# Two unused tiles ahead of the matmul operands: moving tile starts to multiples of 512 bytes

## The chip, the cores and the metric

The kernel is one program on one core of a Trainium2 chip. The metric is the device time of one execution in microseconds (us). The kernel before has a median of 947.3 us over three runs (946.58 to 951.47).

## The reference, cut to what matters

One layer of a hybrid decoder on 512 tokens of 1024 channels in float32: half a SwiGLU feed-forward step, a mixer of two groups (a convolution of 31 taps with a layer norm, and a gated linear recurrence), another half feed-forward step, and a last RMS norm.

```
def swiglu_ffn(x, w_gate, w_up, w_down):
    return (jax.nn.silu(x @ w_gate) * (x @ w_up)) @ w_down

x = x + 0.5 * swiglu_ffn(rmsnorm(x, ffn1_norm), ffn1_w_gate, ffn1_w_up, ffn1_w_down)
x = x + hybrid_mixer(rmsnorm(x, mix_norm), w_in, ..., w_out)
x = x + 0.5 * swiglu_ffn(rmsnorm(x, ffn2_norm), ffn2_w_gate, ffn2_w_up, ffn2_w_down)
y = rmsnorm(x, final_norm)
```

The inner width of the feed-forward steps is 2816, that is 22 feature tiles of 128. The mixer's input product has 2048 outputs, its output product 1024.

## The kernel before, in words

Every large product is made of three matmuls in float32r (a 4-byte type that TensorE reads in one pass). Both operands are split into a high part, rounded to float32r, and a low part, the rest; the product is high by high, high by low and low by high, all added up in one PSUM bank.

There are two kinds of these matmuls. In `mm_feat` (line 194) the weights are stationary and the tokens move: the stationary operand is a block of 128 by 128 of a weight slab `hl`, the moving operand a row of 512 or 256 tokens of `h_hi` or `h_lo`, the normed and transposed input. One unit is 24 such matmuls, 8 blocks times 3 products, into one bank (`pgate`, `pup` in the feed-forward steps, `pz` in the mixer). In `mm_tok` (lines 329, 330, 331) the activations are stationary and the weights move: the stationary operand is a block of 128 by 128 of an `act`, `uhi`, `ulo`, `yhi` or `ylo` tile, the moving operand 512 columns of a slab `hl`. Its outputs are called `pd`, and `pdl` at the program's end.

Counted in the built program, the 4656 float32r matmuls are 1584 of `mm_feat` with 512 columns, 1056 of `mm_feat` with 256 columns into `pgate` and `pup` (the first units, and those of the second feed-forward step that take half of the tokens at a time), 768 with 256 columns into `pz`, and 1248 of `mm_tok`, all with 512 columns.

A weight slab goes through three stages: a DMA of 512 KB into a tile `raw` (SyncE's queue), a cast of ScalarE into the high half of `hl` (line 119), and a subtraction on VectorE or GpSimd into its low half (line 133). Three `raw` and five `hl` tiles are in rotation, and the program writes these stages ahead of the unit that uses the slab by fixed numbers of units. The order on each engine comes from the order of the code and from priorities that the program gives to chains of small steps (norms, the convolution, the recurrence).

The tiles come from pools that lay them out one behind the other in each partition of the on-chip memory, in the order of the pools: first the persistent tiles (`const`), then `raw` and `hl`, then the working tiles, `act` among them. A tile's place is the sum of the sizes ahead of it, each rounded up to 32 bytes. So nothing is computed or moved by a tile that nobody reads or writes; it shifts what lies behind it.

| tile | byte in the partition, before | remainder by 512 | role in the large matmuls |
|---|---|---|---|
| `xt0` to `xt3` | 16512 and on | 128 | none |
| `h_hi`, `h_lo` | 32896, 49280 | 128 | moving in `mm_feat` |
| `ident`, `ones` | 65664, 66176 | 128 | none |
| `raw` | 88544 and on | 480 | none (DMA target) |
| `hl` | 100832 and on | 480 | stationary in `mm_feat`, moving in `mm_tok` |
| `act`, `uhi`, `ulo`, `yhi`, `ylo` | 149984 and on | 480 | stationary in `mm_tok` |

The blocks that one matmul reads begin at whole multiples of 512 bytes within their tile, so a tile's remainder is that of all its blocks.

Of the kernel before, what the change touches and what calls it, by code (L numbers as in the profile page):

```python
# [13 lines left out]
P = 128  # L14
# [44 lines left out]
def layer_kernel(ctx: ExitStack, tc, x, gains, w_g1, w_u1, w_d1a, w_d1b, w_in,  # L59
# [16 lines left out]
    def const(shape, name, dt=F32):  # L76
        return cp.tile(shape, dt, name=name, tag=name)

# [1 line left out]
    xt = [const([P, D], f"xt{t}") for t in range(4)]  # L80
    h_hi = const([P, KT, T], "h_hi", F32R)
    h_lo = const([P, KT, T], "h_lo", F32R)
    ident = const([P, P], "ident")
    ones = const([P, P], "ones")
    neghalf = const([P, 1], "neghalf")
# [16 lines left out]
        nc.sync.dma_start(g, gains[i:i + 1, :].broadcast_to([P, D]))  # L102
        return g

# [1 line left out]
    clock = {"pe": 0.0, "dve": 0.0, "pool": 0.0}  # L106
    chains, convs, done = [], [], {}

    def dve(us):
        clock["dve"] = max(clock["dve"], clock["pe"] - 3.0) + us  # L110

    # slabs are loaded, then split into two parts of float32r
    def slab_load(st, src):
        st["raw"] = wp.tile([P, D], F32, name=nm("raw"), tag="raw", bufs=RAW_BUFS)
        nc.sync.dma_start(st["raw"], src)
# [69 lines left out]
            if evac is not None:  # L185
                evac()

# [1 line left out]
    def mm_feat(ps, hl, t0, n):  # L189
        w = hl.rearrange("p s (k f) -> p s k f", k=KT)  # L190
        seq = [(0, h_hi), (0, h_lo), (1, h_hi)]
        for s, (a, h) in enumerate(seq):
            for k in range(KT):
                PE.matmul(ps, w[:, a, k, :], h[:, k, t0:t0 + n],  # L194
                          start=(s == 0 and k == 0), stop=(s == 2 and k == KT - 1))
# [5 lines left out]
            tc.keep_in_program_order(ins)  # L201
        return ins

    # a bank for the products beside the main ones
    def side_tile(name):
        if "free" in done:
            return pd.tile([P, T], F32, name=nm(name), tag="pd")
        return pp.tile([P, T], F32, name=nm(name), tag="pg")

# [1 line left out]
    def m4(name, dt=F32):  # L211
        return sp.tile([P, 4, HT], dt, name=nm(name), tag="act", bufs=ACT_BUFS)

# [58 lines left out]
        if key is not None:  # L272
            done[key] = True

# [1 line left out]
    def ffn_units(acts, j, wg, wu, parts, shared=False):  # L276
        box = {}

        def gate(t0, n, hl):
            if hl is not None:  # L280
                box["g"] = hl
            pg = pp.tile([P, T], F32, name=nm("pgate"), tag="pg")
            mm_feat(pg[:, :n], box["g"], t0, n)
            box["pg"] = pg

        def gate_out(t0, n):
            pg = box["pg"]
            sg = sp.tile([P, T], F32, name=nm("sg"), tag="sg", bufs=2)
            S.activation(sg[:, :n], pg[:, :n], AF.Silu)  # L289
            box["s"] = sg  # L290

        def up(t0, n, hl):
            if hl is not None:
                box["u"] = hl
            pu = pp.tile([P, T], F32, name=nm("pup"), tag="pg")
            mm_feat(pu[:, :n], box["u"], t0, n)
            box["pu"] = pu

        def up_out(t0, n):
            pu = box["pu"]  # L300
            sg = box["s"]
            act = acts[j]
            V.tensor_mul(sg[:, :n], pu[:, :n], sg[:, :n])  # L303
            S.copy(act[:, 0, t0:t0 + n], sg[:, :n])
            V.tensor_sub(act[:, 1, t0:t0 + n], sg[:, :n], act[:, 0, t0:t0 + n].bitcast(F32))  # L305
            dve(0.8 if n == 256 else 1.3)

        out_ = []
        for i, (t0, n) in enumerate(parts):
            us = 5.12 * n / 512  # L310
            out_.append((wg[j] if i == 0 else None, shared, us,
                         lambda hl, t0=t0, n=n: gate(t0, n, hl),
                         lambda t0=t0, n=n: gate_out(t0, n)))
            out_.append((wu[j] if i == 0 else None, shared, us,
                         lambda hl, t0=t0, n=n: up(t0, n, hl),
                         lambda t0=t0, n=n: up_out(t0, n)))
        return out_
# [6 lines left out]
            self[j] = new_act()  # L324
            return self[j]

# [1 line left out]
    def mm_tok(ps, ahi, alo, whi, wlo, first, last):  # L328
        PE.matmul(ps, ahi, whi, start=first, stop=False)  # L329
        PE.matmul(ps, ahi, wlo, start=False, stop=False)  # L330
        PE.matmul(ps, alo, whi, start=False, stop=last)  # L331
# [7 lines left out]
    def pd_tile():  # L339
        return pd.tile([P, 512], F32, name=nm("pd"), tag="pd")  # L340

    # down products of the first group of feature tiles, one half of the
    # output columns at a time, all tokens
    def down_a_units(wd, acts):
        box = {}

        def unit(oh, kp, hl):
            if kp == 0:
                box["ps"] = [pd_tile() for _ in range(4)]
            ps = box["ps"]  # L350
            hv = hl.rearrange("p s (j d) -> p s j d", j=2)
            for j in range(2):
                k = 2 * kp + j
                for t in range(4):
                    ts_ = slice(t * P, (t + 1) * P)
                    mm_tok(ps[t], acts[k][:, 0, ts_], acts[k][:, 1, ts_],
                           hv[:, 0, j, :], hv[:, 1, j, :], k == 0, k == NA - 1)

        def fin(oh):
            for t in range(4):  # L360
                add_res(t, oh, box["ps"][t], 0.5)

        return [(wd[oh, kp], False, 5.12, lambda hl, oh=oh, kp=kp: unit(oh, kp, hl),
                 (lambda oh=oh: fin(oh)) if kp == NA // 2 - 1 else None)
                for oh in range(2) for kp in range(NA // 2)]

    # products of two token tiles with the full width of the output
    def pair_units(ws, order, kept, left, toks, scale, shared, after, again=False):
        box = {}
        n = len(order)  # L370

        def unit(i, k, hl):
            if hl is None:
                hl = kept.pop(k)
            elif k in kept:
                kept[k] = hl
            if i == 0:
                done.pop("free", None)
                box["ps"] = [[pd_tile() for _ in range(2)] for _ in range(2)]
            ps = box["ps"]  # L380
            for j in range(2):
                hi, lo = left(k, j)
                for oh in range(2):
                    os_ = slice(oh * 512, (oh + 1) * 512)
                    mm_tok(ps[j][oh], hi, lo, hl[:, 0, os_], hl[:, 1, os_], i == 0, i == n - 1)

        def fin():
            for i, t in enumerate(toks):
                for oh in range(2):
                    add_res(t, oh, box["ps"][i][oh], scale)  # L390
            done["free"] = True
            after()

        return [(None if again and k in kept else ws[k], shared, 2.56,
                 lambda hl, i=i, k=k: unit(i, k, hl), fin if i == n - 1 else None)
                for i, k in enumerate(order)]
# [12 lines left out]
        order = [4, 5, 6, 7, 0, 1, 2, 3] if (YF0, YF1)[half] else list(range(8))  # L409
        return pair_units(w_out, order, {}, left, (2 * half, 2 * half + 1), 1.0, True, after)  # L410

# [1 line left out]
    def par(c, i):  # L413
        return ch[:, c, i:i + 1]

# [93 lines left out]
                    yield 0.4  # L509
        chains.append((PR_LN, layernorm(cv, half)))  # L510

    # mean over the channels, the same in every partition
    def channel_mean(v, box):
        ps2 = sp.tile([P, 2, HT], F32, name=nm("ps2"), tag="sg", bufs=2)
        V.tensor_add(ps2, v[:, 0:2, :], v[:, 2:4, :])
        V.tensor_add(ps2[:, 0, :], ps2[:, 0, :], ps2[:, 1, :])
        dve(1.1)
        for _ in range(NY3):
            yield 1
        pm = side_tile("pm")  # L520
        PE.matmul(pm[:, :HT], ones, ps2[:, 0, :], start=True, stop=True)
        box.append(pm)
# [106 lines left out]
        V.tensor_scalar_mul(psp, q, 8.0)  # L629
        V.tensor_scalar_mul(nsp, q, -8.0)  # L630

# [1 line left out]
    row1 = sp.tile([1, P], F32, name="row1", tag="sg", bufs=2)  # L633
    V.memset(row1, 1.0)
    g1ps = [pd_tile() for _ in range(2)]
# [28 lines left out]
        return lambda: chains.append(  # L664
            (PR_NORM, norm_chain(toks, gains_of[n], f"h{n}{toks[0] // 2}")))

    # the same slabs once more, for the other half of the tokens
    def again_units(first, second):
        out_ = []
        for i, (_, _, us, mm, evac, _) in enumerate(second):  # L670
            box = {}
            first[i][5]["keep"] = box
            out_.append((None, False, us, lambda hl, mm=mm, box=box: mm(box.pop("hl")), evac))
        return out_
# [48 lines left out]
    for j in range(NB):  # L723
        u += ffn_units(b2, j, w_g2[NA:], w_u2[NA:], [ALL])

    # last down products and the final norm
    last = {}

    def final(k, hl):
# [100 lines left out]
```

## Time and profile before

| what | value |
|---|---|
| median of three runs | 947.3 us (946.58 to 951.47) |
| span of the profiled execution | 945.9 us |
| mean granted TensorE clock in it | 0.987 |
| TensorE matmul (PE) busy | 907.8 us, 96% of the span |
| TensorE weight load (PEld) busy | 776.7 us, 82% |
| VectorE (DVE), ScalarE (ACT), GpSimd (POOL) busy | 475.1, 368.6, 210.8 us |
| DMA engines, mean share | 35% for the queue that loads the weights |

In a timeline each row is a stretch of like instructions: its start, how long it lasts from the first start to the last end, engine, line, operation, output and inputs, and how many there are. One matmul's own duration holds the time until its last result is written, which overlaps the next matmul. How fast matmuls follow each other is read from the starts of two rows, divided by the number of matmuls between them; this text calls it the spacing.

### The profile page before, as it was taken

Reading aid. Unit: us, or ns where it says so; the run is one execution under the profiler, and the core shown is the slowest. Engines: PE = TensorE matmul, PEld = TensorE weight load, DVE = VectorE, ACT = ScalarE, POOL = GpSimd, SP = SyncE. Lnnn points to the kernel's source line nnn. Section 1 sums busy time; section 2 is a strip of 40 time slices with the busy share of each in tenths; the row PEclk is TensorE's granted clock in tenths of the full one; section 3 lists DMA queues with packets and bytes.
Section 4 is the critical chain, followed back from the end, with each engine's and each line's share of the span. In section 5 each row is a group of like instructions: output and inputs, shape, how many; then the busy total and the mean of one; then the engine's idle time right before and its main releaser. Section 6 shows DMA issues by size and latency. Waiting matters only on the chain.

```text
span 945.9 us, 11886 instructions
## 1 busy us (share of the span) xinstructions
PE 907.8 (96%) x4796; PEld 776.7 (82%) x4796; DVE 475.1 (50%) x677; ACT 368.6 (39%) x502; POOL 210.8 (22%) x120
## 2 busy tenths in 40 slices
PE   8999999999999999988889798999999999999997
PEld 6988888888888889888878697799988888888885
DVE  6533333333333433989999897555523333333224
ACT  6522221132222334466876554644511222223113
POOL 2000000000000038884856786700000000000001
PEclk9999999999999999998999899999999999999999
DMA  8322222322222344552433444445533222232202
GB/s 273 121 90 99 101 89 93 108 89 89 89 98 103 123 167 149 186 199 99 148 130 119 153 163 150 158 174 181 184 107 111 89 89 89 94 107 89 89 24 89
DMA packets 33401, 115.94 MB, mean 123 GB/s; under 512 B 4673, under 2 KB 4801, under 8 KB 33346
## 3 DMA queue, kind: packets, MB, share of 16 engines
q1 hardware_dynamic: 32770, 114.14, 34.8%
q10 hardware_dynamic: 576, 1.05, 0.3%
q8 instruction: 37, 0.61, 0.3%
q14 instruction: 18, 0.15, 0.0%
HBM read 113.07 MB, written 2.10 MB: 122 GB/s over the span
## 4 chain that ended last, share of the span: by engine, by line
PE 82%; DVE 13%; ACT 1%; DMA 1%; POOL 1%; issue 1%; SPq 0%; POOLq 0%; ACTq 0%; DVEq 0%
PE pgate L194 25%; PE pup L194 24%; PE pd L331 8%; PE pd L329 8%; PE pd L330 8%; PE pz L194 5%; DVE pc L506 4%; DVE xr L462 2%; PE pdl L331 1%; PE pdl L330 1%; PE pdl L329 1%; DVE th L595 1%; DVE xn L226 1%; DVE act L305 1%; DMA raw<-in_w_u 1%
## 5 line engine op out<-in xcount | busy, mean ns | idle before, releaser
L119 ACT CAST hl<-raw 128x1024 fp32r<-128x1024 f32 x208 | 217.7, 1048 | 330.6 <-PE pup L194 149.5
L133 DVE TENSOR_TENSOR hl<-raw,hl 128x1024 fp32r<-128x1024 f32 x136 | 168.2, 1237 | 290.3 <-ACT hl L119 290.3
L133 POOL TENSOR_TENSOR hl<-raw,hl 128x1024 fp32r<-128x1024 f32 x72 | 180.8, 2520 | 390.6 <-ACT hl L119 385.1
L194 PE MATMUL pgate<-h_hi,hl 128*128 128x512 f32 (+1 forms) x880 | 184.6, 352 | 0.8 <-ACT h_hi L246 0.8
L194 PE MATMUL pup<-h_hi,hl 128*128 128x512 f32 (+1 forms) x880 | 184.3, 351 | 0.3 <-DVE sg L303 0.3
L194 PEld LDWEIGHTS pgate<-h_hi,hl 128*128 128x128 f32 x880 | 145.0, 190 | 25.8 <-ACT h_hi L246 1.5
L194 PEld LDWEIGHTS pup<-h_hi,hl 128*128 128x128 f32 x880 | 144.9, 190 | 24.8 <-DVE sg L303 0.5
L329 PE MATMUL pd<-hl,act 128*128 128x512 f32 x304 | 118.4, 390 | 0.0
L331 PE MATMUL pd<-hl,act 128*128 128x512 f32 x304 | 118.3, 389 | 0.0
L330 PE MATMUL pd<-hl,act 128*128 128x512 f32 x304 | 118.3, 389 | 0.0
L506 DVE SCALAR_TENSOR_TENSOR pc<-ub,ch,pc 128x256 f32<-128x256 f32 x232 | 94.6, 477 | 0.0
L194 PE MATMUL pgate<-h_lo,hl 128*128 128x512 f32 (+1 forms) x440 | 92.3, 352 | 1.8 <-DVE h_lo L252 1.8
L194 PE MATMUL pup<-h_lo,hl 128*128 128x512 f32 (+1 forms) x440 | 91.7, 350 | 0.0
L289 ACT ACTIVATE sg<-pgate 128x512 f32<-128x512 f32 (+1 forms) x55 | 28.2, 513 | 159.0 <-PE pgate L194 159.0
L194 PEld LDWEIGHTS pgate<-h_lo,hl 128*128 128x128 f32 x440 | 72.5, 190 | 14.2 <-DVE h_lo L252 2.0
L194 PEld LDWEIGHTS pup<-h_lo,hl 128*128 128x128 f32 x440 | 72.1, 188 | 12.1
L303 DVE TENSOR_TENSOR sg<-pup,sg 128x512 f32<-128x512 f32 (+1 forms) x55 | 32.0, 583 | 94.6 <-PE pup L194 94.6
L758 POOL TENSOR_SCALAR sf<-sf 128x1 f32<-128x1 f32 x4 | 1.2, 300 | 323.7 <-ACT sqo L755 323.7
L194 PE MATMUL pz<-h_hi,hl 128*128 128x256 f32 x512 | 70.4, 287 | 0.0
L331 PEld LDWEIGHTS pd<-hl,act 128*128 128x128 f32 x304 | 57.1, 188 | 11.9
L329 PEld LDWEIGHTS pd<-hl,act 128*128 128x128 f32 x304 | 57.1, 188 | 11.8
L330 PEld LDWEIGHTS pd<-hl,act 128*128 128x128 f32 x304 | 57.1, 188 | 11.7
(118 smaller groups left out, 759.9 us busy)
## 6 DMA issues: line engine op xcount, KB each, us to landing
raw<-in_w_g SPq DMA_DIRECT2D x53, 512.0 KB, 3.2
raw<-in_w_u SPq DMA_DIRECT2D x53, 512.0 KB, 3.2
raw<-in_w_in SPq DMA_DIRECT2D x32, 512.0 KB, 3.2
raw<-in_w_d1b SPq DMA_DIRECT2D x22, 512.0 KB, 3.2
raw<-in_w_out SPq DMA_DIRECT2D x16, 512.0 KB, 3.2
raw<-in_w_d2b SPq DMA_DIRECT2D x12, 512.0 KB, 3.2
raw<-in_w_d1a SPq DMA_DIRECT2D x10, 512.0 KB, 3.2
raw<-in_w_d2a SPq DMA_DIRECT2D x10, 512.0 KB, 3.2
```

The costliest lines, as they stand in the source:

```text
L119: S.copy(st["hl"][:, 0, :], st["raw"])
L133: eng.tensor_sub(st["hl"][:, 1, sl], st["raw"][:, sl], st["hl"][:, 0, sl].bitcast(F32))
L194: PE.matmul(ps, w[:, a, k, :], h[:, k, t0:t0 + n], start=(s == 0 and k == 0), stop=(s == 2 and k == KT - 1))
L226: V.scalar_tensor_tensor(out=xn, in0=xt[t], scalar=ss[:, 1:2], in1=g, op0=ALU.mult, op1=ALU.mult)
L289: S.activation(sg[:, :n], pg[:, :n], AF.Silu)
L303: V.tensor_mul(sg[:, :n], pu[:, :n], sg[:, :n])
L305: V.tensor_sub(act[:, 1, t0:t0 + n], sg[:, :n], act[:, 0, t0:t0 + n].bitcast(F32))
L329: PE.matmul(ps, ahi, whi, start=first, stop=False)
L330: PE.matmul(ps, ahi, wlo, start=False, stop=False)
L331: PE.matmul(ps, alo, whi, start=False, stop=last)
L462: V.scalar_tensor_tensor(out=xr[:, c, :], in0=rxb[:, c, half * HT + k:half * HT + k + HT], scalar=par(c, P_LW + k), in1=xr[:, c, :], op0=A ...
L506: V.scalar_tensor_tensor(out=cv[:, c, :] if j == 30 else acc, in0=src, scalar=par(c, P_DW + j), in1=acc, op0=ALU.mult, op1=ALU.add)
```

## The change

Two tiles are added to the persistent pool: `pad0`, 96 floats (384 bytes) in each partition, between `xt3` and `h_hi`, and `pad1`, 40 floats (160 bytes), between `h_lo` and `ident`. Nothing reads or writes them. The first moves `h_hi` and `h_lo` on by 384 bytes, to 33280 and 49664; both together move everything behind by 544 bytes, `raw` to 89088, `hl` to 101376 and `act` to 150528. All of these are multiples of 512. The last byte in use goes from 228208 to 228752. The rest of the diff takes comments away. Row by row, the instructions on each engine, their operands' names and shapes and their order are the same in both programs.

```
     xt = [const([P, D], f"xt{t}") for t in range(4)]
+    const([P, 96], "pad0")
     h_hi = const([P, KT, T], "h_hi", F32R)
     h_lo = const([P, KT, T], "h_lo", F32R)
+    const([P, 40], "pad1")
     ident = const([P, P], "ident")
```

More of the change, by code (lines that the diff above doesn't have):

```diff
@@ L80, in layer_kernel @@
     xt = [const([P, D], f"xt{t}") for t in range(4)]
+    const([P, 96], "pad0")
     h_hi = const([P, KT, T], "h_hi", F32R)
     h_lo = const([P, KT, T], "h_lo", F32R)
+    const([P, 40], "pad1")
     ident = const([P, P], "ident")
```

## The prediction

> **What bounds the kernel now.** I read the page's busy shares and its chain of waits first.
>
> ```profile
> PE 907.8 (96%) x4796; PEld 776.7 (82%) x4796; DVE 475.1 (50%) x677; ACT 368.6 (39%) x502; POOL 210.8 (22%) x120
> PE 82%; DVE 13%; ACT 1%; DMA 1%; POOL 1%; issue 1%; SPq 0%; POOLq 0%; ACTq 0%; DVEq 0%
> ```
>
> TensorE is busy for 96% of the span and is 82% of the chain that ends last. So the time between one matmul and the next is what counts, and it is counted thousands of times. The table of windows shows where TensorE never stops.
>
> ```profile
> 28.00:112.00 84.00, 84.00 (x408) 69.72 (x407) 32.23 (x50) 25.76 (x35) 0.00 (x0) 1.00 0.29 101
> 152.00:302.00 150.00, 150.00 (x647) 121.34 (x646) 51.48 (x55) 37.70 (x48) 0.00 (x0) 1.00 0.28 95
> 440.00:560.00 120.00, 104.78 (x723) 97.74 (x722) 113.39 (x173) 86.70 (x126) 85.37 (x37) 0.96 0.40 140
> 708.00:858.00 150.00, 150.00 (x647) 121.32 (x646) 50.93 (x55) 38.30 (x48) 0.00 (x0) 1.00 0.28 95
> 858.00:925.00 67.00, 67.00 (x295) 55.11 (x294) 18.83 (x19) 14.12 (x18) 0.51 (x2) 1.00 0.18 63
> ```
>
> After the window's length come busy time and count of PE, PEld, DVE, ACT and POOL, then the granted clock, the DMA share and GB/s. In the feed-forward stages PE fills the window at full clock while VectorE and ScalarE are busy for a third of it or less; only the mixer (here 440 to 560) has gaps. Every nanosecond off a feed-forward matmul's spacing is a nanosecond off the end, and the other engines have room to follow.
>
> Then the spacing itself, from the timeline of PE. First `mm_feat` with 512 columns, then `mm_tok`, then `mm_feat` with 256 columns, once in the feed-forward step and once in the mixer:
>
> ```profile
> 82.13 2.03 PE L194 MATMUL pup<-h_hi,hl 128*128 128x512 f32 x8
> 84.00 2.03 PE L194 MATMUL pgate<-h_hi,hl 128*128 128x512 f32 x8
> 93.37 2.04 PE L194 MATMUL pup<-h_hi,hl 128*128 128x512 f32 x8
> ...
> 505.13 0.39 PE L329 MATMUL pd<-hl,yhi 128*128 128x512 f32 x1
> 509.89 0.39 PE L329 MATMUL pd<-hl,yhi 128*128 128x512 f32 x1
> ...
> 640.18 1.10 PE L194 MATMUL pgate<-h_lo,hl 128*128 128x256 f32 x8
> 654.26 1.10 PE L194 MATMUL pup<-h_lo,hl 128*128 128x256 f32 x8
> ...
> 470.64 2.08 PE L194 MATMUL pz<-h_hi,hl 128*128 128x256 f32 x16
> 473.52 2.08 PE L194 MATMUL pz<-h_hi,hl 128*128 128x256 f32 x16
> ```
>
> - `mm_feat`, 512 columns: from 82.13 to 93.37 there are six groups of 8, 11.24 us / 48 = 234.2 ns. I use 234.
> - `mm_tok`, 512 columns: from 505.13 to 509.89 stand 21 matmuls, 4.76 us / 21 = 226.7 ns.
> - `mm_feat`, 256 columns: 14.08 us / 120 = 117.3 ns in the first stretch, 2.88 us / 24 = 120.0 ns in the second.
>
> What would they be without any stall? When the granted clock is half, the matmuls show it:
>
> ```profile
> 428.90:430.60 1.70, 1.70 (x8) 1.70 (x9) 1.70 (x5) 0.00 (x0) 0.00 (x0) 0.50 0.24 96
> ```
>
> Eight 256-column matmuls in 1.70 us at clock 0.50 are 213 ns each; at full clock that is 106.5, and 213 for 512 columns. So at full clock something stalls every float32r matmul, and not equally: by 21 ns in `mm_feat` with 512 columns, by 13.7 in `mm_tok`, by 11 to 13.5 in `mm_feat` with 256. At half clock the stall is gone, which speaks for reading: at full clock the array takes 4 bytes per column twice as fast. The two 512-column kinds load a block of weights for every matmul, stream as many columns and write one bank; the difference that I find is where their operands lie. In `mm_feat` the moving tile has the remainder 128 by 512 and the stationary one 480; in `mm_tok` both have 480.
>
> **The change part by part.** It removes no instruction and adds none; each engine's rows stand as before. Three things move.
>
> (1) The remainder of the large matmuls' operands: 128 and 480 become 0 and 0 in `mm_feat`, 480 and 480 become 0 and 0 in `mm_tok`. After the change both kinds have what only `mm_tok` had before: both operands start at the same remainder. If the weight load that runs beside each matmul collides with the moving stream by their relative place, `mm_feat` takes on `mm_tok`'s cadence: 1584 x (234.2 - 226.7 ns) = 11.9 us. `mm_tok` itself keeps its relative place and gains nothing. For the 256 columns two cadences were seen at the same remainders; going from 117.3 to 120.0 would cost 1056 x 2.7 ns = 2.9 us, and the reverse for the mixer's 768 would gain 2.1 us at most, where other work covers part of it. I take zero for them and keep +3 and -2 for the range.
>
> What the 512-byte start is worth cannot be read from a row, since no large operand has it. The bounds are the rows themselves: at best all stalls go, (234.2 - 213) x 1584 = 33.6 us, (226.7 - 213) x 1248 = 17.1, (117.3 - 106.5) x 1056 = 11.4, and up to 9 for `pz`: 62 to 71 us, most of it on the path. At worst `mm_tok` takes `mm_feat`'s 234.2: 1248 x 7.5 = 9.4 us, and the 256-column units lock at 120: 12.3 in all. I take -11.9, because it is the one cadence that the trace shows for operands of equal remainder.
>
> The Trainium skill speaks against a collision of the two streams: TensorE: Matmul & The Clock Gate, Step-by-step, has TensorE read through two independent ports, so that loading the next weights takes nothing from the running matmul. By it the sum would be zero. The stalls of 13.7 to 21 ns are more than that page's roughly 2.5 ns per warm matmul, so a cost that it does not name is in this trace.
>
> (2) The `raw` tiles, the DMA's targets, go from 480 to 0. The loads are covered: a 512 KB load lands 3.2 us after its issue, the queue's share is 34.8%, and in the whole list of PE's waits the only DMA is at the start.
>
> ```profile
> raw<-in_w_g SPq DMA_DIRECT2D x53, 512.0 KB, 3.2
> PE pd L637 <- DMA grow<-in_gains: 3.9, 1, 3.9
> ```
>
> Zero; if landing became slower by a whole 3.2 us, SyncE's issue, which stands units ahead of use, would still hide it but for the start, so a few us would be the most.
>
> (3) VectorE, ScalarE and GpSimd read and write at moved starts. They fill a third of the feed-forward windows; zero there. In the mixer VectorE fills 113.39 of 120 us, and a change of 1% in its instructions would be 1 us on the chain.
>
> The sum is 945.9 - 11.9 = 934.0 us for the profiled execution. The median of the runs stands 1.4 us higher, so 935.4, rounded to **935 us**.
>
> **The rivals.**
>
> No change, **947 us**. The cadence is a matter of time, not of place. For it: at the very same remainders the 256-column units run at 117.3 in one stretch and at 120.0 in the other, so the place alone does not set it; and `mm_tok`'s groups of three share stationary blocks and change banks, which `mm_feat`'s do not. And after an interruption `mm_tok` runs some matmuls slower before it settles, at unchanged places:
>
> ```profile
> 499.00 0.39 PE L330 MATMUL pd<-hl,uhi 128*128 128x512 f32 x1
> 501.08 0.39 PE L330 MATMUL pd<-hl,uhi 128*128 128x512 f32 x1
> ```
>
> Those are nine matmuls in 2.08 us, 231 ns each. Against it: undisturbed, `mm_feat` with 512 columns keeps its pace for the whole program, in the chain of waits 5.62 us for 24 (234.2) from the first unit to the last, over other slabs and other layers' inputs, and never falls into 226.7.
>
> ```profile
> 39.18 5.62 PE pgate L194 x24
> 856.98 5.62 PE pup L194 x24
> ```
>  The Trainium skill, SBUF — State Buffer, Specifications (TRN2), has 16-byte lines and a penalty for each crossing to a new one. All tiles stand at multiples of 32 before and after, so by that nothing changes; no run here shows the lines themselves.
>
> All stalls go, **about 885 us**. The stall is a fetch of a larger piece of memory that is split by a start inside it, and the new starts split none. The price is the upper sum above, 62 us; 947.3 - 62 = 885. For it: at half clock the stall is nil. Against it: a split at the start costs each matmul the same, and the stall of `mm_feat` grows from 11 to 21 ns with the columns. A part of it only, say a third to a half, gives 915 to 927.
>
> Slower, **957 us**. Two streams that start at the same place hit the same piece of memory, and what protected `mm_tok` was a start off the boundary (480), not the equality. Then `mm_tok` takes `mm_feat`'s 234.2 and `mm_feat` keeps its own: +9.4 us, 956.7; with the 256-column units at 120.0, 959.6. It decides once `mm_tok`'s spacing passes 226.7 + 4.7 us / 1248 = 230.5 ns. For it: the moving operand nearest to a round start now, `mm_feat`'s 128, has the worse cadence. Against it: nothing else in the trace.
>
> That the change doesn't do what it says is hardly a case: the starts in the built program are multiples of 512.
>
> **How the numbers follow.** `mm_feat` at `mm_tok`'s cadence 0.37, no change 0.32, stalls gone wholly or in good part 0.16, slower 0.15. The likeliest gives 935. A measurement of this kernel tells about 0.5% (4.7 us) from no change. Faster by more: 0.37 + 0.16, less a little for gains too small, 0.51. Slower by more: 0.15. Within: 0.34. The range from 912 to 955 holds the likeliest (931 to 940 with the bounds of the 256-column units), no change, a part of the large gain and the small half of the slower case; it leaves out the full 885 and the worst of the slower ones. The likeliest case's own range is 931 to 940.
>
> **What would show it.** In the profile after: rows of eight `mm_feat` matmuls 1.81 us apart instead of 1.87 show step (1); 226.7 in `mm_tok` shows that equality counts and the absolute place does not. Both spacings as before say that place plays no part. Under 220 ns in both would be the split fetch; over 230.5 in `mm_tok` the slower rival. Step (2) is wrong if PE waits for `raw` or for ScalarE's cast. The prediction as a whole is wrong if PE's windows from 28 to 395 us take as long as now.

## The result, and the profile after

The changed kernel takes **938.8 us**, the median of five runs (936.67 to 940.54); the kernel before took 949.0 us, also the median of five runs (946.58 to 951.47), three of which are those that gave the 947.3 above. The ratio is 0.9893, with a 95% interval of 0.9867 to 0.9918: faster by 1.1%, between 0.8 and 1.3. The profiled execution of the changed kernel has a span of 937.1 us, against 945.9 before, at a granted clock of 0.985 against 0.987.

The page of the changed kernel, busy shares and the chain that ends last:

```profile
PE 898.5 (96%) x4796; PEld 778.1 (83%) x4796; DVE 475.0 (51%) x677; ACT 368.4 (39%) x502; POOL 211.0 (23%) x120
PE 81%; DVE 13%; DMA 2%; issue 1%; POOL 1%; ACT 1%; SPq 0%; POOLq 0%; ACTq 0%; DVEq 0%
```

PE's busy time falls by 9.3 us (907.8 to 898.5) with the same 4796 matmuls; that is the whole gain of the span (8.8). VectorE, ScalarE and GpSimd stay within 0.2 us of what they were. The table of windows of the changed kernel, in the same stretches as before:

```profile
152.00:302.00 150.00, 150.00 (x664) 124.20 (x663) 51.98 (x56) 40.51 (x50) 0.00 (x0) 1.00 0.29 95
440.00:560.00 120.00, 104.17 (x720) 97.45 (x719) 112.58 (x172) 81.86 (x115) 87.36 (x38) 0.96 0.43 142
708.00:858.00 150.00, 150.00 (x663) 124.22 (x662) 51.24 (x54) 39.82 (x50) 0.00 (x0) 1.00 0.29 96
```

PE is still busy without a break in the two feed-forward windows, at the same full clock, but 664 and 663 matmuls fit where 647 did. In the mixer's window little changes: PE is busy for 104.17 us of it where it was 104.78, with 720 matmuls where it had 723. The spacing, from PE's timeline of the changed kernel: `mm_feat` with 512 columns (now line 196), `mm_tok`, and `mm_feat` with 256 columns.

```profile
81.13 1.98 PE L196 MATMUL pgate<-h_hi,hl 128*128 128x512 f32 x8
82.94 1.98 PE L196 MATMUL pgate<-h_lo,hl 128*128 128x512 f32 x8
...
92.01 1.98 PE L196 MATMUL pgate<-h_hi,hl 128*128 128x512 f32 x8
...
500.12 0.39 PE L331 MATMUL pd<-hl,yhi 128*128 128x512 f32 x1
...
506.92 0.39 PE L331 MATMUL pd<-hl,yhi 128*128 128x512 f32 x1
...
629.95 1.12 PE L196 MATMUL pgate<-h_hi,hl 128*128 128x256 f32 x8
...
649.15 1.12 PE L196 MATMUL pup<-h_lo,hl 128*128 128x256 f32 x8
```

- `mm_feat`, 512 columns: 81.13 to 92.01 are six groups of 8, 10.88 us / 48 = 226.7 ns, where it was 234.2.
- `mm_tok`: 500.12 to 506.92 are 30 matmuls, 6.80 us / 30 = 226.7 ns, as before.
- `mm_feat`, 256 columns: 629.95 to 649.15 are twenty groups of 8, 19.20 us / 160 = 120.0 ns, where a stretch of before had 117.3.

A unit of 24 matmuls in the chain that ended last takes 5.44 us where it took 5.62:

```profile
48.65 5.44 PE pgate L196 x24
97.61 5.44 PE pup L196 x24
```

The spacings of all matmuls, from each start to the next, added up by kind:

| kind | matmuls | before, us | after, us | difference | mean spacing before, after (full clock), ns |
|---|---|---|---|---|---|
| `mm_feat`, 512 columns | 1584 | 371.1 | 359.1 | -12.0 | 234.28, 226.70 |
| `mm_feat`, 256, `pgate` and `pup` | 1056 | 129.7 | 131.4 | +1.7 | 117.8, 119.95 |
| `mm_feat`, 256, `pz` | 768 | 113.0 | 113.2 | +0.2 | 118.6, 120.0 |
| `mm_tok` | 1248 | 296.2 | 297.8 | +1.6 | 226.96, 226.95 |
| the small ones | 140 | 24.9 | 24.3 | -0.6 | - |

That makes -9.1; the first matmul starts 0.3 us later, which leaves the 8.8 us of the span. The +1.6 of `mm_tok` is not its cadence, which is unchanged, but more matmuls at half clock: 33 of its spacings are longer than 260 ns, 23 before, and 14 of the 33 are 426 or 427 ns, twice the 213 that the prediction took for 512 columns at full clock, against 6 before. The table of windows shows the granted clock in the output products at the end of the mixer, where they are, of the changed kernel:

```profile
560.00:623.00 63.00, 57.88 (x342) 51.13 (x341) 40.70 (x63) 32.01 (x47) 34.68 (x17) 0.95 0.50 166
```

There it is 0.95 (the third number from the end). The same window of the kernel before and of experiment 1 below, whose instructions stand in the same order:

```profile
560.00:623.00 63.00, 57.75 (x380) 52.35 (x379) 46.10 (x79) 34.69 (x50) 40.05 (x20) 0.97 0.50 171
```

```profile
560.00:623.00 63.00, 57.92 (x359) 51.35 (x359) 42.01 (x67) 34.11 (x49) 35.16 (x18) 1.00 0.51 168
```

So this term is a matter of the clock that an execution was granted there. That the placement has no part in it is not shown by itself; experiment 1, with the same spacings, did without it.

The waits of PE in the changed kernel hold nothing new. The longest of them, engine, line, what it waited for, then us in total, times, and the longest:

```profile
PE pz L196 <- DVE h_lo L254: 5.9, 1, 5.9
PE pm L523 <- DVE ps L518: 5.5, 3, 2.9
PE ptr L244 <- DVE xn L228: 4.8, 1, 4.8
PE pd L639 <- DMA grow<-in_gains: 4.2, 1, 4.2
```

No wait for `raw` or for the cast stands in the list; the only DMA is the one at the start, 4.2 us where it was 3.9.

The chain that ended last does run through loads of `raw` in the mixer, each followed by ScalarE's cast. Its rows (start, us, what) for the kernel before, with one such load between 440 and 560 us:

```profile
508.80 3.22 DMA raw<-in_w_in
```

and for the changed kernel, with a second one:

```profile
500.38 3.15 DMA raw<-in_w_in
539.33 4.86 DMA raw<-in_w_g
```

The second one is in the chain of experiment 1 as well, with 3.98 us. What it costs is not shown by itself; PE's busy time between 440 and 560 us is 0.6 us less than before in the changed kernel and 0.1 less in experiment 1 (104.68).

### The profile page after: what moved, and what is told of

Same layout as the page of the kernel before. It is cut to its first block, busy times and chain, and to the rows that moved or that the text cites. A ratio compares the mean times of both kernels' runs of the same rounds, so it can differ in the third digit from the quotient of the medians.

```text
span 937.1 us, 11886 instructions
## 1 busy us (share of the span) xinstructions
PE 898.5 (96%) x4796; PEld 778.1 (83%) x4796; DVE 475.0 (51%) x677; ACT 368.4 (39%) x502; POOL 211.0 (23%) x120
## 4 chain that ended last, share of the span: by engine, by line
PE 81%; DVE 13%; DMA 2%; issue 1%; POOL 1%; ACT 1%; SPq 0%; POOLq 0%; ACTq 0%; DVEq 0%
PE pgate L196 24%; PE pup L196 24%; PE pd L333 8%; PE pd L331 8%; PE pd L332 8%; PE pz L196 5%; DVE pc L508 4%; DVE xr L464 2%; PE pdl L332 1%; PE pdl L331 1%; PE pdl L333 1%; DVE th L597 1%; DVE xn L228 1%; POOL hl L135 1%; DMA raw<-in_w_u 1%
## 5 line engine op out<-in xcount | busy, mean ns | idle before, releaser
L196 PE MATMUL pup<-h_hi,hl 128*128 128x512 f32 (+1 forms) x880 | 180.4, 347 | 1.4 <-DVE sg L305 1.4
L196 PE MATMUL pgate<-h_hi,hl 128*128 128x512 f32 (+1 forms) x880 | 180.7, 347 | 0.6 <-ACT h_hi L248 0.6
L332 PE MATMUL pd<-hl,act 128*128 128x512 f32 x304 | 118.3, 389 | 0.0
L333 PE MATMUL pd<-hl,act 128*128 128x512 f32 x304 | 118.3, 389 | 0.0
L196 PE MATMUL pgate<-h_lo,hl 128*128 128x512 f32 (+1 forms) x440 | 90.3, 347 | 1.9 <-DVE h_lo L254 1.9
L333 PEld LDWEIGHTS pd<-hl,act 128*128 128x128 f32 x304 | 57.1, 188 | 11.8
L196 PEld LDWEIGHTS pz<-h_hi,hl 128*128 128x128 f32 x512 | 66.5, 196 | 0.4
L331 PEld LDWEIGHTS pd<-hl,act 128*128 128x128 f32 x304 | 57.1, 188 | 11.8
```

Of the source, the lines that this page charges most:

```text
L196: PE.matmul(ps, w[:, a, k, :], h[:, k, t0:t0 + n], start=(s == 0 and k == 0), stop=(s == 2 and k == KT - 1))
```

## The experiments

The theory to be tested: what counts is the distance between the start of the moving operand and that of the stationary one. Its first rival: what counts is that an operand starts at a multiple of 512 bytes, as the change is described. Its second rival: the cadence is a matter of order and time, and the new places met it by chance. Experiments 3 to 7 and 9 have one run each, and the 13 runs of the kernel before beside experiments 1 to 4 lie between 944.8 and 950.8 us; so there the spacings carry the argument, and the time only has to agree with them.

**1. Only the second tile.** `h_hi` and `h_lo` stay at 128 by 512, and everything behind moves by 160 bytes, so `hl` and `act` come to 128 as well. The distance is zero, and no operand of a large matmul starts at a multiple of 512.

```
-    const([P, 96], "pad0")
     h_hi = const([P, KT, T], "h_hi", F32R)
     h_lo = const([P, KT, T], "h_lo", F32R)
     const([P, 40], "pad1")
```

> Only the second tile (160 bytes behind h_lo): h stays at remainder 128 by 512, hl and act go to 128. No large operand begins at a multiple of 512, but in every matmul both operands have the same remainder. Relative theory (what counts is the distance between the starts of the moving and the stationary operand): mm_feat with 512 columns at 226.7 ns as in the changed kernel, 256 columns at 120.0, mm_tok 226.7; time about 939 us, ratio 0.989. Rival, absolute theory (a start inside a 512-byte piece costs): mm_feat stays at 234.3 since its moving start stays at 128, time about 949, ratio 1.00.

Measured: 935.8 us, median of four runs, ratio to before 0.9876 (0.9848 to 0.9904). Timeline of PE of this kernel:

```profile
83.04 1.98 PE L195 MATMUL pgate<-h_hi,hl 128*128 128x512 f32 x8
...
93.92 1.98 PE L195 MATMUL pgate<-h_hi,hl 128*128 128x512 f32 x8
```

Six groups of 8 in 10.88 us: 226.7 ns. The 256-column units are at 120.0 and `mm_tok` at 226.9, all as in the changed kernel. So one tile of 160 bytes brings the whole gain, and the start at a multiple of 512 plays no part in it.

**2. Only the first tile.** `h_hi` and `h_lo` start at multiples of 512; `hl` and `act` move by 384 bytes to 352, so the distance stays 352, as before.

```
     const([P, 96], "pad0")
     h_hi = const([P, KT, T], "h_hi", F32R)
     h_lo = const([P, KT, T], "h_lo", F32R)
-    const([P, 40], "pad1")
```

> Only the first tile (384 bytes ahead of h_hi): the moving operand of mm_feat begins at multiples of 512, its stationary operand hl goes to remainder 352, so the distance stays 352 as in the kernel before; act goes to 352 as well. Relative theory: mm_feat with 512 columns stays at 234.3 ns, mm_tok 226.7, time about 949 us, ratio 1.00. Absolute theory, moving start: mm_feat 226.7, time about 939, ratio 0.989; absolute theory, stationary start: as before.

Measured: 947.2 us, median of ten runs, ratio 0.9998 (0.9978 to 1.0019). Timeline of PE of this kernel:

```profile
82.13 2.04 PE L195 MATMUL pup<-h_hi,hl 128*128 128x512 f32 x8
...
93.37 1.80 PE L195 MATMUL pup<-h_hi,hl 128*128 128x512 f32 x7
```

11.24 us for 48: 234.2 ns, as in the rows of before (the last row shows 7 of its 8 matmuls, as the view ends there). The moving operand's multiple of 512 alone is worth nothing. The two runs together refute the first rival.

**3. Only the activations moved away.** A third unused tile of 352 bytes stands ahead of the working tiles of the changed kernel, so that `act`, `uhi`, `ulo`, `yhi` and `ylo` start at 352 by 512; `hl` and `h` stay at 0. Nothing changes for `mm_feat`; in `mm_tok` the moving operand stays at a multiple of 512 and the stationary one is 352 bytes off.

```
+    sp.tile([P, 88], F32, name="pad2", tag="pad2", bufs=1)
```

> The changed kernel with a third unused tile of 352 bytes ahead of the working tiles: act, uhi, yhi and the like go to remainder 352, hl and h stay at 0. In mm_tok the distance (stationary minus moving) is now 352, as in mm_feat before. Relative theory: mm_tok goes from 226.7 to about 234.3 ns, 1248 x 7.6 = 9.5 us slower than the changed kernel, about 948 us; mm_feat stays at 226.7. Absolute theory: mm_tok's moving operand stays at a multiple of 512 and nothing changes, about 939 us (the kernel before had mm_tok's stationary operand off the multiple too, at 226.7).

Measured: 948.7 us in one run, beside 948.5 for the kernel before, and a span of 946.9 us. Timeline of PE, `mm_tok` in the last output products:

```profile
900.61 0.39 PE L332 MATMUL pd<-hl,act 128*128 128x512 f32 x1
...
904.13 0.40 PE L332 MATMUL pdl<-hl,act 128*128 128x512 f32 x1
```

15 matmuls in 3.52 us: 234.7 ns; over the program 234.27, which was `mm_feat`'s cadence before. `mm_feat` with 512 columns keeps 226.7. The sum of `mm_tok`'s spacings grows to 306.7 us, 8.9 more than in the changed kernel, and the span by 9.8. So the cadence of 234 can be brought to the other kind of matmul by the distance alone, in the same order of instructions. That refutes the second rival, and it shows that `mm_feat` is not special: either kind is slow at a distance of 352. Whether a matmul's moving operand is to be compared with its own stationary block or with the block that is loaded for the next matmul cannot be told, since all blocks of a tile have the same remainder.

**4. The distance 256.** `pad1` of the changed kernel grows to 416 bytes: `hl` and `act` start at 256 by 512, `h` at 0. In `mm_tok` the distance stays zero.

```
-    const([P, 40], "pad1")
+    const([P, 104], "pad1")
```

> The changed kernel with the second tile 256 bytes larger: h at 0, hl and act at remainder 256, distance 256 in mm_feat and 0 in mm_tok. Relative theory with a period of 512 bytes: mm_feat leaves 226.7 ns for another cadence between 213 and 240; with a period of 256 or less (256, 128, 64): mm_feat stays at 226.7, about 939 us. mm_tok at 226.7 in either. Absolute theory by the moving start in mm_feat: 226.7 there.

Measured: 938.4 us in one run, span 936.7. Timeline of PE of this kernel:

```profile
82.21 1.97 PE L196 MATMUL pgate<-h_hi,hl 128*128 128x512 f32 x8
...
87.65 1.98 PE L196 MATMUL pup<-h_hi,hl 128*128 128x512 f32 x8
```

5.44 us for 24: 226.7 ns. A distance of 256 is as good as none. So whatever repeats does so at 256 bytes or at a divisor of that, not at 512.

**5. and 6. Five distances in one program.** Each of the five `hl` tiles is made 32 bytes longer, so that the five slabs are 0, 32, 64, 96 and 128 bytes away from the moving operand; in the second kernel the view of the slab begins 16 bytes into the tile (`4:4 + 2 * D`), which gives 16, 48, 80, 112 and 144. In `mm_tok` the distances are the negatives of these. The third tile of experiment 3 is in both kernels, as the rest behind needs it.

```
-        st["hl"] = wp.tile([P, 2, D], F32R, name=nm("hl"), tag="hl", bufs=HL_BUFS)
+        hl = wp.tile([P, 2 * D + 8], F32R, name=nm("hl"), tag="hl", bufs=HL_BUFS)
+        st["hl"] = hl[:, 0:2 * D].rearrange("p (s d) -> p s d", s=2)
```

> The five hl tiles are 32 bytes longer each, so they begin at remainders 0, 32, 64, 96 and 128 by 512 while h and act stay at 0: one run shows five distances, +0 to +128 in mm_feat and 0 to -128 in mm_tok, by unit. Relative theory with a period of 64 bytes (256 acted like 0, 352 = 5 x 64 + 32 did not): units on slabs at 0, 64 and 128 run at 226.7 ns, those at 32 and 96 at 234.3, in both kinds; 2 of 5 units slow, about 2828 x 0.4 x 7.6 ns = 8.6 us over the changed kernel, 947 us. Period 128: 0 and 128 at 226.7 only, 32, 64 and 96 slower, about 952 us. Period 256: only 0 at 226.7. Rival, a fixed cost of each weight load with no regard to place: no difference by slab (the earlier runs speak against it).

> As the run with slabs 32 bytes apart, and in addition the halves of each slab begin 16 bytes into the tile: distances 16, 48, 80, 112 and 144 in mm_feat, the same negative in mm_tok. If 16-byte lines are all that counts, and the distance by 32 is what matters between them, 16 should be like one of its neighbours (226.7 or 234.3). If the stall varies smoothly with the distance, something between 213 and 240 other than these two, perhaps below 226.7. Time between 935 and 955 us.

Measured: 951.7 us (span 949.9) and 954.0 us (span 952.3), one run each, beside 945.5 for the kernel before. A time alone would not tell one period from another; the spacings of `mm_feat`, sorted by the slab's distance, do (means in ns; the row for 256 columns takes `pgate`, `pup` and `pz` together):

| distance, bytes | 0 | 16 | 32 | 48 | 64 | 80 | 96 | 112 | 128 | 144 |
|---|---|---|---|---|---|---|---|---|---|---|
| `mm_feat`, 512 columns | 228.0 | 229.7 | 233.2 | 233.0 | 233.3 | 232.1 | 234.0 | 233.3 | 232.4 | 227.4 |
| `mm_feat`, 256 columns | 119.9 | 119.1 | 118.1 | 118.3 | 114.9 | 119.1 | 117.7 | 119.7 | 118.8 | 119.5 |

For `mm_tok` the first of the two kernels gives 228.6 at 0, and 233.2, 229.8, 233.4 and 232.2 at -32, -64, -96 and -128.

Timeline of PE of the first of the two kernels; the slab of the unit that begins at 182.04 has the distance 0, that of the one at 193.10 the distance 96:

```profile
182.04 2.01 PE L198 MATMUL pgate<-h_hi,hl 128*128 128x512 f32 x8
183.89 1.98 PE L198 MATMUL pgate<-h_lo,hl 128*128 128x512 f32 x8
185.70 1.98 PE L198 MATMUL pgate<-h_hi,hl 128*128 128x512 f32 x8
...
193.10 2.03 PE L198 MATMUL pgate<-h_hi,hl 128*128 128x512 f32 x8
194.98 2.03 PE L198 MATMUL pgate<-h_lo,hl 128*128 128x512 f32 x8
196.85 2.04 PE L198 MATMUL pgate<-h_hi,hl 128*128 128x512 f32 x8
```

At distance 0 the first group of 8 takes 1.85 us, 231 ns each, and the second 1.81, 226 each: it needs some matmuls to settle after the unit before it. At 96 two groups take 3.75 us, 234 each. Since neither 32, 64 nor 128 reach 226.7 and 256 does, the period is 256 bytes; and 96, which is 352 less 256, has the spacing of the kernel before (234.0 against 234.28). The distances from 32 to 128 lie at 232 to 234, and none of the ten has a cadence below 226.7 that holds for 512 columns in `mm_feat`. Zero and 256 are not the only good ones, though: 144 has a mean of 227.4, and 16 one of 229.7.

The table's means hide that one distance can have two cadences. Timeline of PE of the second kernel, two units whose slabs both have the distance 16, the first of them right behind `mm_tok`:

```profile
182.10 2.03 PE L198 MATMUL pgate<-h_hi,hl 128*128 128x512 f32 x8
183.97 2.03 PE L198 MATMUL pgate<-h_lo,hl 128*128 128x512 f32 x8
...
210.06 1.98 PE L198 MATMUL pup<-h_hi,hl 128*128 128x512 f32 x8
211.87 1.98 PE L198 MATMUL pup<-h_lo,hl 128*128 128x512 f32 x8
```

The first takes 1.87 us for 8, 234 ns each, the second 1.81, 226 each. At 144 the same is seen: the one unit that follows such a slow one runs at 233, the others begin at 226.7. So at 16 and 144 what came before goes with one or the other of two cadences; at 0 and at 256, after settling, only 226.7 was seen.

**7. Half of the weight load.** If the weight load that runs beside a matmul takes the moving stream's place, a load of half as many columns should take less of it. In the changed kernel the 8 matmuls of each 512-column unit that use `h_lo` load 64 instead of 128 columns; that half of the high by low product is left out.

```
+                m = 64 if s == 1 and n == T else P
-                PE.matmul(ps, w[:, a, k, :], h[:, k, t0:t0 + n],
+                PE.matmul(ps[:m], w[:, a, k, :m], h[:, k, t0:t0 + n],
```

> The changed kernel, but the 8 high-by-low matmuls of each 512-column mm_feat unit (528 in all) load only 64 of the 128 stationary columns and write 64 partitions; half of that product is left out. Relative theory in the form that the weight load collides with the moving stream: with half of the load the stall of 13.4 ns over 213.3 shrinks in these matmuls, to about 6.7 (220 ns), 528 x 6.7 ns = 3.5 us less, about 935 us. Rival, a fixed cost of changing weights: stays at 226.7 ns, 939 us. Fewer columns that cost more by a change of shape would show at the first and last of the eight only.

Measured: 943.8 us in one run, span 942.0, against 938.8 and 937.1 for the changed kernel, of which the sum of `mm_feat`'s spacings below explains 3.5 us. Timeline of PE of this kernel:

```profile
81.67 1.98 PE L197 MATMUL pgate<-h_hi,hl 128*128 128x512 f32 x8
83.48 2.00 PE L197 MATMUL pgate<-h_lo,hl 128*64 128x512 f32 x8
85.33 2.00 PE L197 MATMUL pgate<-h_hi,hl 128*128 128x512 f32 x8
87.16 1.98 PE L197 MATMUL pup<-h_hi,hl 128*128 128x512 f32 x8
```

The eight with the half load take 1.85 us, 231 ns each, against 1.81 (226) for the eight ahead of them, and the next eight with full loads 1.83. Over the program it is 230.6 for the 528 with the half load and 228.1 for the other 1056: 3.5 us in all. The stall did not shrink with the load, and this run does not bear out a plain competition for bandwidth between load and stream. It does not refute one either, since with the change of shape the full loads behind became slower too (228.1 against 226.7).

**8. Zero for 512 columns, 64 for 256.** Experiment 5 had its best 256-column spacing at the distance 64 (114.9). This kernel has no unused tiles; the `hl` tiles are 8448 bytes apart, 33 times 256, and every 512-column matmul has the distance 0 by 256. The slabs of the 256-column units begin 64 bytes into their tile. To make room, the small tiles of the norms' sums are parts of two persistent tiles.

```
-        st["hl"] = wp.tile([P, 2, D], F32R, name=nm("hl"), tag="hl", bufs=HL_BUFS)
+        hl = wp.tile([P, 2 * D + 64], F32R, name=nm("hl"), tag="hl", bufs=HL_BUFS)
+        st["hl"] = hl[:, by:by + 2 * D].rearrange("p (s d) -> p s d", s=2)
...
-                         lambda hl, t0=t0, n=n: gate(t0, n, hl),
+                         shift(lambda hl, t0=t0, n=n: gate(t0, n, hl), 64 if n == HT else 0),
```

> A version that sets the distance by kind: no pads; hl tiles 8448 bytes apart (33 x 256), so that with h at 128 by 256 every 512-column matmul of both kinds has distance 0 by 256; in the units with 256 columns the halves of the slab begin 64 bytes into the tile, distance 64. The room comes from packing the small statistics tiles together. Same instructions in the same order on PE. Theory (distance by 256 bytes sets the cadence): 512 columns 226.7 ns in both kinds, 256 columns at 113.5 or 117.8 (both were seen at 64) instead of 120.0. Over the changed kernel 1056 x 6.5 ns = 6.9 us in the feed-forward step and up to 768 x 6.5 = 5 us in the mixer at 113.5, so 927 to 932 us; at 117.8 about 2.3 + 1.7 us, 934 to 937. Rival, the cadence of a unit is set by how it starts and not by the distance: 120.0 stays and the time is that of the changed kernel, about 938.

Measured: 935.5 us, median of six runs (933.03 to 939.79), ratio to before 0.9883 (0.9859 to 0.9907); the profiled execution has a span of 931.3 us. Timeline of PE of this kernel:

```profile
614.08 1.98 PE L210 MATMUL pgate<-h_lo,hl 128*128 128x512 f32 x8
...
621.33 1.98 PE L210 MATMUL pup<-h_hi,hl 128*128 128x512 f32 x8
623.14 1.10 PE L210 MATMUL pgate<-h_hi,hl 128*128 128x256 f32 x8
...
673.08 1.11 PE L210 MATMUL pup<-h_hi,hl 128*128 128x256 f32 x8
```

An earlier stretch of the same kernel, with the same distance of 64:

```profile
529.11 1.07 PE L210 MATMUL pgate<-h_hi,hl 128*128 128x256 f32 x8
...
542.71 1.07 PE L210 MATMUL pup<-h_hi,hl 128*128 128x256 f32 x8
```

512 columns: 7.25 us / 32 = 226.6 ns. 256 columns: 53 groups in 49.94 us / 424 = 117.8 ns in the late stretch, and 15 groups in 13.60 us / 120 = 113.3 ns in the early one. So this distance has two cadences, and the late stretch stands in the higher one throughout. Over the program the 256-column units of the feed-forward steps are at 115.7 ns on average, 127.0 us in all, 4.4 less than in the changed kernel. This kernel is faster than the one before; its interval overlaps the changed kernel's (0.9867 to 0.9918), so that it beats that one is not shown.

**9. Other distances for 256 columns.** As in 8, with the feed-forward's 256-column units at 160, 192, 224, 176, 208, 240, 64, 72 and 56 bytes, by feature tile, and `pz` at 0.

```
-                         shift(lambda hl, t0=t0, n=n: gate(t0, n, hl), 64 if n == HT else 0),
+                         shift(lambda hl, t0=t0, n=n: gate(t0, n, hl), (160, 192, 224, 176, 208, 240, 64, 72, 56)[j % 9] if n == HT else 0),
```

> As the version that sets the distance by kind, but in the 256-column units of the feed-forward steps the distance differs by feature tile: 160, 192, 224, 176, 208, 240, 64, 72 and 56 bytes, and the mixer's units stay at 0. Theory: each distance has its own cadences between 107 and 120 ns, 64 again 113.5 or 117.8, mixer at 120.0. It tells whether a distance is better than 64. Rival: no dependence on the distance, 120.0 throughout. Time 930 to 938 us.

Measured: 936.9 us in one run, span 935.1. Mean spacing of 256 columns by distance by 256: 0 at 120.0, 56 at 117.7, 64 at 113.7, 72 at 118.4, 160 at 119.9, 176 at 118.1, 192 at 115.6, 208 at 116.8, 224 at 116.7, 240 at 120.0. 64 and 192 are the two that settle at 113.3, and 192 also shows 117.8, as 64 does in experiment 8; 8 bytes off 64 the 113.3 is gone. None of the distances tried is better.

## Why the prediction was right, and where not

**What bounds the kernel.** Right: the gain of the span, 8.8 us, is the loss of PE's busy time (9.3), and no other engine turned up as the bound.

**Step (1), `mm_feat` takes `mm_tok`'s cadence: -11.9 us.** Measured -12.0: 1584 x 7.58 ns. That `mm_tok` gains nothing was right too (226.96 to 226.95 ns). The reason, the relative place of the two operands and not their start, is shown by experiment 1, where equal places off the multiples of 512 bring the whole gain, by 2, where a start at a multiple of 512 with unequal places brings none, and by 3, where the other kind of matmul is made slow. The prediction held a rule against it: by the Trainium skill, TensorE: Matmul & The Clock Gate, Step-by-step, loading the next weights takes nothing from the running matmul. By that rule alone the gain would have been zero, and it was not: with one and the same order of instructions the distance between the two operands is worth 7.6 ns for each matmul. Whether it is the load that takes this time from the matmul is not shown. The 16-byte lines that the Trainium skill gives under SBUF — State Buffer, Specifications (TRN2), do not explain the difference either: in experiment 5 all starts are multiples of 32 bytes, and the means at the distances 0 and 96 differ by 6 ns.

What collides is only argued. For a collision of load and stream speaks that the spacing depends on the distance between them, and that at half clock it does not: 512 columns take 427 ns there in `mm_tok` of the changed kernel (distance 0) and of experiment 3 (distance 352) alike. Experiment 7, with half the load, did not show the stall shrink. Why the period is 256 bytes, and why 13.4 ns (226.7 - 213.3) remain at distance zero, stays open.

**The 256-column units, taken as zero.** This is the term that was mis-sized: +1.7 us for `pgate` and `pup`, within the bound of +3. The two cadences of before, 117.3 and 120.0 in the rows, average 117.8; at distance zero 996 of 1056 spacings are 120. The prediction named this direction and then took zero, because the trace of before showed both cadences at one distance. For `pz` the same lock adds about 1 us (118.6 to 120.0 ns), and its spacings around waits and at half clock came out some 0.8 us shorter in this execution, which leaves +0.2 in the sum.

**Steps (2) and (3), zero.** Right as far as the profile shows: no wait of PE for `raw` appeared, the other engines' busy time is unchanged, and the mixer's window fills PE for 104.17 of 120 us, against 104.78. The prediction looked at PE's waits alone; the chain through the mixer holds loads of `raw`, before and after, so "covered" is shown for PE and not for every engine.

**The sum.** 934.0 us were worked out for the profiled execution, which took 937.1. The 3.1 us between are the 256-column units (+1.7), the matmuls at half clock (+1.6), `pz` (+0.2) and the later start (+0.3), less the small matmuls (-0.6) and the 0.1 by which step (1) gave more. The half clock was not in the prediction; the window 560 to 623 shows 0.97, 0.95 and 1.00 in three profiles of programs with the same order. Four runs of experiment 1, whose cadences are the changed kernel's, have their median at 935.8. Between the medians taken beside each other the change gained 10.2 us (949.0 to 938.8), where 12.3 were forecast (947.3 to 935).

Two figures of the prediction do not follow from its rows. With the 120.0 ns that it shows for `pz` the most that this term could gain is 768 x 13.5 = 10.4 us, not 9. And with its own bounds of -2.1 and +2.9 us the likeliest case lies between 933.3 and 938.3, not 931 and 940; the measured 938.8 is inside the second and half a microsecond above the first.

**The rivals.** No change: refuted, but its evidence was real. One distance can have two cadences (16 and 144 bytes for 512 columns, 64 for 256), so the place alone does not always set it; for 512 columns at zero and at 96 it does. All stalls go: refuted, for at multiples of 512 the spacing is 226.7 and not 213. Slower, because two streams at the same place collide: refuted, `mm_tok` at 0 and 0 stays at 226.95, below the 230.5 from which it would have decided. That rival had the sign of the effect the wrong way round: for 512 columns equal places are among the good ones.

## What to carry to other kernels

When float32r matmuls follow each other without a break and one kind is slower per column than another, compare the starts of the stationary and the moving operand in the partition, by 256 bytes: in this kernel an unused tile of 160 bytes that makes the difference zero was worth 7.6 ns of 234 for each 512-column matmul. Alignment of each operand by itself bought nothing, and 256-column matmuls preferred another distance, so look at each kind's spacing in the timeline before and after, not at the placement rule. Here the gain lay in stretches that TensorE fills without a break; in the mixer, where it waits for other engines, the change of `pz`'s spacing left the sum within 0.2 us.

## What the runs showed of the hardware that was not expected

- The spacing of 512-column float32r matmuls at full clock depends on the distance between the two operands with a period of 256 bytes: 226.7 ns at 0 and 256, 234.0 and 234.3 at 96 and 352.
- For 256 columns it goes the other way: 120.0 ns at zero, 113.3 or 117.8 at 64 and 192, means of 116.7 to 120.0 at the other distances tried.
- One place can hold two cadences, and the matmuls can keep one of them for long, over 424 in experiment 8; after a change of distance some pass before it settles: in the unit of experiment 5 that begins at 182.04 the first eight average 231 ns, the next eight 226.
- At half clock 512 columns take 427 ns at the distances 0 and 352 alike.
- Loading 64 instead of 128 stationary columns made those matmuls slower, 230.6 against 226.7 ns, and the ones behind them too, 228.1.
